# Head 1's keys and queries by seven products, the replaced block of x made in the gate stage, and weight sums in halves

## The chip, the cores and the metric

One NeuronCore of one Trainium2 chip runs the whole kernel. The metric is the device time of one launch in microseconds; a kernel's figure is the median of several executions. The engines are called PE (TensorE, matrix products), DVE (VectorE), ACT (ScalarE), POOL (GpSimd) and SP (SyncE). SP, ACT and POOL also issue transfers (DMAs); a queue's instructions run in order.

## What is computed

One layer of a hybrid decoder trunk on 512 tokens with 16 learned meta tokens ahead of them, all in float32, D = 2048:

```python
h = rms_norm(x, norm_w)
proj = h @ w_in
(dq, dk, dv, dz, db, da, gq, gk, gv, gz, gl, fq, fk, fv, fz, ff) = split_cols(proj)
...
o_dn = gated_head_norm(o_dn, dz, dn_norm_w)        # gated DeltaNet, 6 heads x 128
...
o_gla = gated_head_norm(o_gla, gz, gla_norm_w)     # GLA, 5 heads, keys 64, values 128
...
o_fox = o_fox.reshape(fz.shape) * silu(fz)         # forgetting attention, 5 heads x 128
o = concatenate([o_dn, o_gla, o_fox])[:, PAD:]
return x + o @ w_out
```

A final RMS norm follows, without the meta tokens. For this case the columns of `w_in` that matter most are fk, fq, fv and fz (keys, queries, values and gate of each attention head, a block of 128 columns each) and gz (the gates of the five GLA heads).

## The kernel before

**Exact products from two halves.** Each float32 weight block of 2048 x 128 comes in two raw tiles of 128 x 1024 (`load_half`, L144). SP loads the tile (L147), ACT casts it to a shorter format, `whi` (L165), and DVE subtracts to get the rest, `wlo` (L166); x is held as `xh` and `xl` in the same way, 16 tiles of 128 x 528 tokens. A projection (`inproj`, L254, with matmuls at L240) adds three products: whi x xh, whi x xl, wlo x xh. A block is 48 matmuls of 512 tokens, or 96 of 264 where the meta tokens are needed. Raw, whi and wlo tiles have two buffers each, so a half's split can begin when the half before the last is through PE.

**Seven products for two blocks.** `inproj_pair` (L558) makes two blocks together with seven half-size products (L571), each 24 matmuls of 264 tokens and one weight tile, where a plain pair would need eight. Four of its weight tiles are sums of blocks (`ti`). They are made in DRAM by POOL's DMAs: copies (L492) and accumulating transfers (L490), listed by `in_jobs` and cut into steps by `steps_of` (L485). `load_half` hands them out as it goes: each load adds `rate` to a budget and each step costs 1 or 1.6. `AHEAD` (L1276) starts this after the first gates with a rate of 1.4. The sums for the output projection (`tw`) follow in the same list. Three token sums (t1, t2, t4) are made by `x_sums`. One product needs a "replaced" block: for the 264 upper tokens, x of channel tile k+8 less x of tile k, written over `xh` and `xl` of tile k (k < 8) by `x_last` (L542) once nothing else reads those columns. For each k it loads two blocks (POOL, L546), scales one (ACT, L548), combines (DVE, L549), casts (ACT, L553) and takes the rest (DVE, L554).

**The order of the work.** DeltaNet's two groups of heads come first, then the gz gates of GLA (five projections of 512 tokens, each followed by `gate_z`: evacuation on DVE, a clamp on POOL at L385, three steps on ACT, one product on DVE, all on tiles `zgz` and `stgz`). During these gates DVE runs the elimination of the second DeltaNet group, a string of small operations on the tile `ab` (L740, L742). Its result goes through DRAM: ACT issues `sc` (L744), then `iv` (L747) and `xm` (L749), which wait for `sc`. Then come the projections of GLA in three pairs of heads (`gla_pair`, L957), then head 0 of attention with plain projections, then head 1's keys and queries plain too (`fk`, `fq`, called at the end of head 0 in `fox_head`, L1150), then `x_last`, then seven pairs: head 1's values and gate, and two pairs for each of heads 2, 3 and 4. Then follows the output projection (`pa`, `pq`, `ps`, `pt`, `pr`).

**What sets the order.** A scheduler with a model of its own fixes each engine's order when the kernel is built. The table `PLACE` (L197) says behind which matmul of a projection the small score matmuls of GLA stand: `"pss23": (('fk', 1), 60)` puts those of pair 2, level 3, behind the 60th matmul of fk of head 1. `paced` (L172) fixes that a weight sum's DMA stands behind the current split on POOL's queue, without a wait on a semaphore.

Of the kernel before, what the change touches and what calls it, by code (L numbers as in the profile page):

```python
# [18 lines left out]
P = 128  # L19
# [17 lines left out]
SKIP = 1  # L37
# [45 lines left out]
def tile_hybrid_trunk(ctx, tc, xT, xtok, mtok, w_gate, w_in, w_out, w_dn, consts, lmask, fin_w, out, dbg=None):  # L83
# [13 lines left out]
    def row(name, dt=F32):  # L97
        return wk.tile([P, 3 + T], dt, tag="row", bufs=7, name=name)
# [94 lines left out]
    def part(name, n=512):  # L193
# [11 lines left out]
        "pg00": (('gk', 2), 60),  # L205
        "pss10": (('fk', 0), 84),
# [278 lines left out]
    def steps_of(jobs):  # L485

        nonlocal ready
        for kind, out_, in_ in jobs:
            if kind:
                paced(G.dma_start(out=out_, in_=in_, accum_op=ALU.add, max_dma_last_dim=2048))  # L490
            else:
                x = G.dma_start(out=out_, in_=in_)  # L492
                paced(x)
                if ready < 4:
                    ready += 1
                    tc.add_manual_dep(x.ins, maxes[0].name, mybir.DependencyInfo(
                        mybir.DependencyClass.NoSync, mybir.DependencyReason.DATA), reason="behind")
            yield 1.6 if kind else 1
# [42 lines left out]

    def x_last():  # L542

        for k in range(NK):
            r = row(f"xe{k}")[:, :T]
            nc.gpsimd.dma_start(out=r.rearrange("p (i t) -> p i t", i=2), in_=xT[:, k : k + 9 : 8, HT:])  # L546
            x12, x22 = r[:, :HT], r[:, HT:]
            A.activation(x12, x12, AF.Copy, scale=nwc[:, k : k + 1])  # L548
            x = V.scalar_tensor_tensor(out=x22, in0=x22, scalar=nwc[:, k + 8 : k + 9], in1=x12, op0=ALU.mult,  # L549
                                       op1=ALU.subtract)  # L550
            tc.add_manual_dep(x.ins, kqs[-1].name, mybir.DependencyInfo(
                mybir.DependencyClass.NoSync, mybir.DependencyReason.DATA), reason="behind")
            A.copy(xh[k][:, HT:], x22)  # L553
            V.tensor_tensor(out=xl[k][:, HT:], in0=x22, in1=xh[k][:, HT:].bitcast(F32), op=ALU.subtract)  # L554
# [3 lines left out]
    def inproj_pair(n, c1, c2, each=None):  # L558
# [6 lines left out]
        def product(p_, src, xx, first=False, cols=slice(0, HT)):  # L565

            third[0] += 1
            hi, lo = load_half(src, f"{b1}_{len(order)}", raws[0] if third[0] % 3 == 0 and 0 < n and h < FOX_HEADS - 1 else None)
# [7 lines left out]
            if each:  # L576
# [16 lines left out]
        product(a, ti[n, 2], xs_(up, hi_))  # L593
        A.copy(c2[:, hi_], a[:, :HT])
        V.scalar_tensor_tensor(out=c2[:, hi_], in0=d[:, :HT], scalar=-1.0, in1=c2[:, hi_], op0=ALU.mult,
                               op1=ALU.subtract)
# [3 lines left out]
        product(a, w_in[b2, 1], sums("t4"), cols=dead)  # L600
        A.activation(c2[:, dead], a[:, dead], AF.Copy, scale=-1.0)
# [355 lines left out]
    def gla_pair(p):  # L957
# [52 lines left out]
        def scores(s, li):  # L1010
# [8 lines left out]
            V.tensor_tensor(out=dv[:, :, 1, :], in0=gv[:, :, 1, :], in1=ref, op=ALU.subtract)  # L1019
# [7 lines left out]
            kqs.append(V.tensor_tensor(out=qxv[:, :, 1, :], in0=qv[:, :, 1, :], in1=dv[:, :, 1, :], op=ALU.mult).ins)  # L1027
# [122 lines left out]
    def fox_head(h):  # L1150
# [125 lines left out]
    AHEAD = {(0, -1): (1.4, (-1, -2, -3, -4, -5, -6, -7), (0, 1, 2, 3))}  # L1276
# [366 lines left out]
```

## Time and profile before

| | us |
|---|---|
| median of 3 runs (lowest, highest) | 1001.61 (999.29, 1006.35) |
| the profiled execution | 997.56 |
| its span, first to last instruction | 995.9 |
| granted TensorE clock in it | 0.997 |
| DVE, ACT, POOL busy | 666.8, 475.3, 249.0 |

The profiled execution is 4.05 us below the median, and 1.7 us of it lie outside its span. The page gives for each engine the busy time, its share of the span and the number of instructions; then groups of instructions by line of the program, tile and shape. In the waits, "A <- B: total, times, longest" says how long A's engine stood idle until B ended. In a timeline a row is start, duration, engine, line, operation, and in brackets the idle time ahead of it with what ended it. In the chain, a row is start, duration, and what ran; a DMA there lasts from its issue until its landing was seen.

### The profile page before, as it was taken

What the parts mean: (1) busy time and instruction counts of PE and PEld (TensorE: products, weight loads), DVE (VectorE), ACT (ScalarE), POOL (GpSimd) and SP (SyncE); (2) the same over time, 40 slices, a digit from 0 to 9 for tenths busy, and PEclk for the clock granted to TensorE, in tenths of its full rate; (3) what the DMA queues carried; (4) which work ended last, traced back from release to release, by engine and by line L of the source; (5) the groups of instructions that cost most, each with busy time, mean ns of one, the idle gap of its engine ahead of it and who ended that gap; (6) DMA issues with size and microseconds to landing.
All of it is one profiled execution on the core that took longest, in us unless ns stands there. A gap on an engine that the chain in (4) does not pass through costs nothing.

```text
span 995.9 us, 19769 instructions
## 1 busy us (share of the span) xinstructions
PE 980.4 (98%) x7774; PEld 896.6 (90%) x7774; DVE 666.8 (67%) x1443; ACT 475.3 (48%) x1043; POOL 249.0 (25%) x293
## 2 busy tenths in 40 slices
PE   9999999999999999999999999999999999999996
PEld 7899999899999888899999988799999998888885
DVE  6356786966567895434675847776766676877573
ACT  7653533334456234334546444555555554454353
POOL 0031423322233244301313223221221134000060
PEclk9999999999999999999999999999999999999998
DMA  9754666777547688844847866565454577355634
GB/s 346 263 193 168 210 216 238 172 181 173 116 113 169 140 215 198 298 130 144 209 143 190 186 178 178 176 200 161 168 172 135 182 267 273 106 190 199 202 106 169
DMA packets 67489, 186.05 MB, mean 187 GB/s; under 512 B 13725, under 2 KB 16973, under 8 KB 66692
## 3 DMA queue, kind: packets, MB, share of 16 engines
q1 hardware_dynamic: 41920, 121.86, 36.0%
q0 software_dynamic: 16576, 56.83, 23.9%
q10 hardware_dynamic: 8900, 6.10, 2.2%
q8 instruction: 61, 1.00, 0.4%
q14 instruction: 32, 0.26, 0.1%
HBM read 174.07 MB, written 56.69 MB: 232 GB/s over the span
## 4 chain that ended last, share of the span: by engine, by line
PE 70%; DVE 7%; DMA 5%; ACT 3%; issue 2%; POOL 1%; ACTq 0%; DVEq 0%; POOLq 0%
PE pp L240 28%; PE pp_a L571 8%; PE pa L1392 5%; PE pq L1392 4%; PE pt L1392 4%; PE ps L1392 2%; PE pp_b L571 2%; PE pp_d L571 2%; PE pp_c L571 2%; DVE wlo L166 2%; DMA sc<-ab 1%; DMA zd<-gqk 1%; PE pr L1392 1%; PE pss L1041 1%; ACT whi L165 1%
## 5 line engine op out<-in xcount | busy, mean ns | idle before, releaser
L240 PE MATMUL pp<-xh,wlo 128*128 128x264 f32 (+2 forms) x1120 | 272.9, 306 | 2.2 <-DVE wlo L166 2.2
L240 PE MATMUL pp<-xh,whi 128*128 128x264 f32 (+2 forms) x1120 | 273.9, 306 | 0.0
L240 PE MATMUL pp<-xl,whi 128*128 128x264 f32 (+2 forms) x1120 | 272.9, 306 | 0.0
L165 ACT CAST whi<-raw 128x1024 fp32r<-128x1024 f32 x131 | 137.1, 1047 | 157.0 <-PE pp L240 81.2
L166 DVE TENSOR_TENSOR wlo<-raw,whi 128x1024 fp32r<-128x1024 f32 x131 | 160.6, 1226 | 72.8 <-ACT whi L165 64.2
L240 PEld LDWEIGHTS pp<-xh,wlo 128*128 128x128 f32 x1120 | 182.6, 189 | 12.1 <-DVE wlo L166 3.6
L240 PEld LDWEIGHTS pp<-xh,whi 128*128 128x128 f32 x1120 | 182.6, 189 | 9.4 <-ACT whi L165 0.4
L240 PEld LDWEIGHTS pp<-xl,whi 128*128 128x128 f32 x1120 | 182.7, 189 | 8.9 <-issue 0.4
L385 POOL TENSOR_SCALAR stc<-cv 128x528 f32<-128x528 f32 (+1 forms) x18 | 28.9, 1607 | 144.9 <-DVE cv L613 124.4
L613 DVE SCALAR_TENSOR_TENSOR cv<-pb,cpk,cv 128x528 f32<-128x528 f32 (+1 forms) x54 | 41.1, 761 | 0.8
L1417 POOL TENSOR_TENSOR acc<-acc,fw 128x512 f32<-128x512 f32 x4 | 5.8, 1483 | 117.4 <-ACT sqf L1414 117.4
L571 PE MATMUL pp_a<-t,whi 128*128 128x264 f32 (+1 forms) x224 | 30.5, 284 | 0.0
L1392 PE MATMUL pa<-wloo,oh 128*128 128x512 f32 x72 | 28.7, 398 | 0.0
L571 PE MATMUL pp_a<-xh,whi 128*128 128x264 f32 x112 | 28.4, 288 | 0.0
L571 PEld LDWEIGHTS pp_a<-t,whi 128*128 128x128 f32 x224 | 27.9, 189 | 0.5
L1392 PE MATMUL pa<-whio,ol 128*128 128x512 f32 x72 | 28.4, 394 | 0.0
L571 PE MATMUL pp_a<-xl,whi 128*128 128x264 f32 x112 | 28.3, 287 | 0.0
L385 POOL TENSOR_SCALAR stdz<-zdz 128x512 f32<-128x512 f32 x6 | 11.3, 1885 | 62.1 <-DVE zdz L403 62.0
L165 ACT CAST whis<-raws 128x1024 fp32r<-128x1024 f32 x16 | 16.3, 1048 | 21.2 <-PE pq L1392 10.8
L166 DVE TENSOR_TENSOR wlos<-raws,whis 128x1024 fp32r<-128x1024 f32 x16 | 19.2, 1223 | 10.7 <-ACT whis L165 10.6
L1392 PE MATMUL pa<-whio,oh 128*128 128x512 f32 x72 | 26.0, 400 | 0.0
L740 DVE TENSOR_TENSOR ab<-ab 51x30 f32<-51x30 f32 (+14 forms) x60 | 21.2, 354 | 6.4 <-DMA ab<-scr 4.2
(509 smaller groups left out, 2138.6 us busy)
## 6 DMA issues: line engine op xcount, KB each, us to landing
raw<-in_w_in SPq DMA_DIRECT2D x103, 512.0 KB, 3.7
ti<-in_w_in POOLq DMA_DIRECT2D x42, 512.0 KB, 5.5
raw<-ti SPq DMA_DIRECT2D x28, 512.0 KB, 3.3
tw<-in_w_dn POOLq DMA_DIRECT2D x24, 512.0 KB, 5.9
ti<-ti POOLq DMA_DIRECT2D x14, 512.0 KB, 6.3
rawo<-in_w_out SPq DMA_DIRECT2D x13, 512.0 KB, 3.2
raws<-tw SPq DMA_DIRECT2D x12, 512.0 KB, 3.9
xt<-in_xtok SPq DMA_DIRECT2D x8, 512.0 KB, 8.9
```

What stands on the lines that cost most here:

```text
L165: pace[0] = A.copy(hi, raw).ins
L166: pace[1] = V.tensor_tensor(out=lo, in0=raw, in1=hi.bitcast(F32), op=ALU.subtract).ins
L240: mm = PE.matmul(p_[:, :nt], wt[:, j * m : (j + 1) * m], xx[k][:, t0 : t0 + nt], start=(k == 0 and wt is hi and xx is xh), stop=(k == KT - ...
L385: maxes.append(G.tensor_scalar_max(t, src, LOW).ins)
L571: m = PE.matmul(p_[:, cols], wt[:, j * P : (j + 1) * P], xx[j][part_][:, cols], start=first and i == 0, stop=i == len(todo) - 1, skip_grou ...
L613: V.scalar_tensor_tensor(out=c, in0=pb[:, t0 + w : w + T], scalar=cwc[:, blk, w : w + 1], in1=c, op0=ALU.mult, op1=ALU.add)
L740: V.tensor_tensor(out=t3, in0=a3[:, j + 1 :, j : j + 1].to_broadcast([NN * 4 + H, m, j]), in1=a3[:, j : j + 1, 0:j].to_broadcast([NN * 4 + ...
L1041: mm = PE.matmul(ps[o0 : o0 + n, b * n : b * n + n], kx[rr, k0 : k0 + n], qx[rr, q0 : q0 + n], start=True, stop=True)
L1392: mm = PE.matmul(p_, o_[:, s], w_, start=(first and n == 0), stop=(last and n == 2), skip_group_check=True)
L1417: G.tensor_tensor(out=acc[tb, cc], in0=acc[tb, cc], in1=fw[cc], op=ALU.mult)
```

## The change

- `SKIP` goes from 1 to 0: head 1's keys and queries are made by seven products too, as pair 0 of now eight. In that pair the replaced product comes last, the product of the dead columns has a bank of its own, and the third raw buffer serves from pair 2 on.
- The replaced blocks are made in `x_early`, two, two, two, one and one after the five gz gates, and stored by POOL to a DRAM tile `x3`. `x_last` is now 16 loads from `x3`, called behind the matmuls of fz of head 0.
- Each DMA of a weight sum becomes two of 64 rows each, and each half waits on a semaphore for the DVE half of the split beside it (`pace[1]`). The rate becomes 1.65, steps cost 0.5 and 0.8, and an eighth pair is in the list.
- `PLACE` moves the scores of GLA's third pair of heads into attention's pair 1.

```diff
-SKIP = 1
+SKIP = 0
...
+        "pss21": (('pair', 1), 22),
...
+        "pss26": (('pair', 1), 102),
+        "pg02": (('pair', 1), 118),
...
-        "pss23": (('fk', 1), 60),
-        "pss24": (('fk', 1), 80),
-        "pss25": (('fk', 1), 90),
-        "pgo2": (('pair', 0), 8),
...
-            if kind:
-                paced(G.dma_start(out=out_, in_=in_, accum_op=ALU.add, max_dma_last_dim=2048))
-            else:
-                x = G.dma_start(out=out_, in_=in_)
-                paced(x)
...
-            yield 1.6 if kind else 1
+            for s in (slice(0, 64), slice(64, P)):
+                if kind:
+                    x = G.dma_start(out=out_[s], in_=in_[s], accum_op=ALU.add, max_dma_last_dim=2048)
+                else:
+                    x = G.dma_start(out=out_[s], in_=in_[s])
...
+                tc.add_manual_dep(x.ins, pace[1].name, mybir.DependencyInfo(
+                    mybir.DependencyClass.Sync, mybir.DependencyReason.DATA), reason="paced")
+                yield 0.8 if kind else 0.5
...
+    x3 = drp.tile([NK, P, T], F32, name="x3")
+
+    def x_early(k):
+
+        r, c = row(f"xe{k}")[:, :T], row(f"xc{k}", F32R)[:, :T]
+        nc.gpsimd.dma_start(out=r.rearrange("p (i t) -> p i t", i=2), in_=xT[:, k : k + 9 : 8, HT:])
+        x12, x22 = r[:, :HT], r[:, HT:]
+        A.activation(x12, x12, AF.Copy, scale=nwc[:, k : k + 1])
+        V.scalar_tensor_tensor(out=x22, in0=x22, scalar=nwc[:, k + 8 : k + 9], in1=x12, op0=ALU.mult,
+                               op1=ALU.subtract)
+        A.copy(c[:, :HT], x22)
+        V.tensor_tensor(out=c[:, HT:], in0=x22, in1=c[:, :HT].bitcast(F32), op=ALU.subtract)
+        nc.gpsimd.dma_start(out=x3[k], in_=c.bitcast(F32))
+
     def x_last():
 
         for k in range(NK):
-            r = row(f"xe{k}")[:, :T]
...
-            A.copy(xh[k][:, HT:], x22)
-            V.tensor_tensor(out=xl[k][:, HT:], in0=x22, in1=xh[k][:, HT:].bitcast(F32), op=ALU.subtract)
+            for x, o in ((xh, 0), (xl, HT)):
+                nc.gpsimd.dma_start(out=x[k][:, HT:].bitcast(F32), in_=x3[k][:, o : o + HT])
...
-            hi, lo = load_half(src, f"{b1}_{len(order)}", raws[0] if third[0] % 3 == 0 and 0 < n and h < FOX_HEADS - 1 else None)
+            hi, lo = load_half(src, f"{b1}_{len(order)}", raws[0] if third[0] % 3 == 0 and 1 < n and h < FOX_HEADS - 1 else None)
...
+        if n > 0:
+            product(a, w_in[b2, 1], sums("t4"), cols=dead)
+            A.activation(c2[:, dead], a[:, dead], AF.Copy, scale=-1.0)
+        else:
+            e = bank("e")
+            product(e, w_in[b2, 1], sums("t4"), True, cols=dead)
+            A.copy(c2[:, dead], e[:, dead])
+            replaced()
+            V.scalar_tensor_tensor(out=c2[:, dead], in0=a[:, dead], scalar=-1.0, in1=c2[:, dead],
+                                   op0=ALU.mult, op1=ALU.subtract)
...
         if h < H1:
...
+            done["fz", h] = inproj(("fz", h), meta=False)
+            x_last()
             gate_z("fz", h)
-            evac(inproj(("fk", H1)), ahead_[H1][:, 0])
-            evac(inproj(("fq", H1), meta=False), ahead_[H1][:, 2], scale=float(P) ** -0.5)
-            x_last()
             claim(h + 1)
...
-    AHEAD = {(0, -1): (1.4, (-1, -2, -3, -4, -5, -6, -7), (0, 1, 2, 3))}
+    AHEAD = {(0, -1): (1.65, (-1, -2, -3, -4, -5, -6, -7, -8), (0, 1, 2, 3))}
...
         gate_z("gz", h)
+        for i in ((0, 1), (2, 3), (4, 5), (6,), (7,))[h]:
+            x_early(i)
```

By the two orders, PE has 48 matmuls fewer of 512 columns, 48 more of 264 and 24 more of 248. There are three raw loads and splits more. Weight sums take 192 DMAs of half the size where there were 88.

The two orders differ most in the stage of the gz gates. First ACT's queue there, before: `whi` is the cast of a weight tile, `stgz` a gate's three steps, `sc`, `iv` and `xm` the way of the elimination through memory.

```order
L165 CAST whi_0_4873<-raw_0_4871 128x1024
L165 CAST whi_1_4904<-raw_1_4902 128x1024
L386 ACTIVATE stgz_4863<-stgz_4863 128x512
L744 DMA sc_4143<-ab_4071 51x1024
L387 ACTIVATE stgz_4863<-stgz_4863 128x512
L388 ACTIVATE stgz_4863<-stgz_4863 128x512
L165 CAST whi_0_4951<-raw_0_4949 128x1024
L747 DMA iv_4145<-sc_4143 128x12x32
L749 DMA xm_4147<-sc_4143 32x3x32
L165 CAST whi_1_5006<-raw_1_5004 128x1024
```

The same place after the change:

```order
L165 CAST whi_1_4950<-raw_1_4948 128x1024
L554 ACTIVATE xe_4817<-xe_4817,cpk 128x264
L557 CAST xc_4818<-xe_4817 128x264
L165 CAST whi_0_5000<-raw_0_4998 128x1024
L389 ACTIVATE stgz_4892<-stgz_4892 128x512
L390 ACTIVATE stgz_4892<-stgz_4892 128x512
L391 ACTIVATE stgz_4892<-stgz_4892 128x512
L165 CAST whi_1_5033<-raw_1_5031 128x1024
L554 ACTIVATE xe_4899<-xe_4899,cpk 128x264
L557 CAST xc_4900<-xe_4899 128x264
L767 DMA sc_4205<-ab_4133 51x1024
L165 CAST whi_0_5089<-raw_0_5087 128x1024
```

Ahead of nearly every `whi` of these gates now stands a block's scale (`xe`) and cast (`xc`), whose inputs come by a DMA and through DVE. The two issues behind `sc` are followed by a block too:

```order
L770 DMA iv_4207<-sc_4205 128x12x32
L772 DMA xm_4209<-sc_4205 32x3x32
L554 ACTIVATE xe_4907<-xe_4907,cpk 128x264
L557 CAST xc_4908<-xe_4907 128x264
L165 CAST whi_1_5145<-raw_1_5143 128x1024
```

POOL's queue in the same stage, before, with the clamps (`stgz`) and the accumulating transfers (`ti`):

```order
L385 TENSOR_SCALAR stc_4065<-cv_4060 128x512
L385 TENSOR_SCALAR stgz_4648<-zgz_4646 128x512
L490 DMA ti<-ti 256x512 x2
L385 TENSOR_SCALAR stgz_4719<-zgz_4717 128x512
L490 DMA ti<-ti 256x512 x2
L385 TENSOR_SCALAR stgz_4791<-zgz_4789 128x512
L490 DMA ti<-ti 256x512 x2
L385 TENSOR_SCALAR stgz_4863<-zgz_4861 128x512
```

And after:

```order
L559 DMA x_683<-xc_4720 128x528
L494 DMA ti<-ti 128x512 x2
L388 TENSOR_SCALAR stgz_4802<-zgz_4800 128x512
L552 DMA xe_4809<-in_xT 128x2x264
L559 DMA x_683<-xc_4728 128x528
L494 DMA ti<-ti 128x512 x2
L552 DMA xe_4817<-in_xT 128x2x264
L559 DMA x_683<-xc_4810 128x528
L494 DMA ti<-ti 128x512 x2
L388 TENSOR_SCALAR stgz_4892<-zgz_4890 128x512
L552 DMA xe_4899<-in_xT 128x2x264
L559 DMA x_683<-xc_4818 128x528
```

The loads of blocks (`xe`) and the stores (`x_683`, which is the tile `x3`, each behind DVE's last operation on its block) stand between the clamps, with two halves of a sum beside each.

DVE's queue at the end of the elimination, after the change, where L763 and L765 are the elimination's two operations:

```order
L763 TENSOR_TENSOR ab_4133<-ab_4133 51x58
L765 TENSOR_TENSOR ab_4133<-ab_4133 51x2x29
L558 TENSOR_TENSOR xc_4900<-xe_4899,xc_4900 128x264
L763 TENSOR_TENSOR ab_4133<-ab_4133 51x30
L765 TENSOR_TENSOR ab_4133<-ab_4133 51x30
L166 TENSOR_TENSOR wlo_0_5090<-raw_0_5087,whi_0_5089 128x1024
L555 SCALAR_TENSOR_TENSOR xe_4907<-xe_4907,cpk 128x264
L406 TENSOR_TENSOR zgz_4980<-pp_0_4915,rstd 128x512
L558 TENSOR_TENSOR xc_4908<-xe_4907,xc_4908 128x264
L166 TENSOR_TENSOR wlo_1_5146<-raw_1_5143,whi_1_5145 128x1024
```

The operations on `xe` and `xc` of the blocks 0 to 4 (ten of them) stand ahead of its last step, and the evacuation `zgz_4980` has moved behind it.

More of the change, by code (lines that the diff above doesn't have):

```diff
@@ L592, in inproj_pair, with replaced @@
         V.tensor_tensor(out=c1[:, hi_], in0=d[:, :HT], in1=c1[:, hi_], op=ALU.add)
[L593 to L596, printed above, removed]
+        def replaced():
+            product(a, ti[n, 2], xs_(up, hi_))
+            A.copy(c2[:, hi_], a[:, :HT])
+            V.scalar_tensor_tensor(out=c2[:, hi_], in0=d[:, :HT], scalar=-1.0, in1=c2[:, hi_], op0=ALU.mult,
+                                   op1=ALU.subtract)
+        if n > 0:
+            replaced()
         c = bank("c")
@@ L599, in inproj_pair @@
         V.tensor_tensor(out=c1[:, hi_], in0=c[:, :HT], in1=c1[:, hi_], op=ALU.add)
-        product(a, w_in[b2, 1], sums("t4"), cols=dead)
-        A.activation(c2[:, dead], a[:, dead], AF.Copy, scale=-1.0)
+        if n > 0:
+            product(a, w_in[b2, 1], sums("t4"), cols=dead)
[4 more added lines that the diff above has]
+            A.copy(c2[:, dead], e[:, dead])
+            replaced()
+            V.scalar_tensor_tensor(out=c2[:, dead], in0=a[:, dead], scalar=-1.0, in1=c2[:, dead],
+                                   op0=ALU.mult, op1=ALU.subtract)
     def conv_silu(key, blk, dst, meta=True):
@@ L1018, in scores @@
             ref = gv[:, :, 0, s - 1 : s].to_broadcast([R, npair, s])
-            V.tensor_tensor(out=dv[:, :, 1, :], in0=gv[:, :, 1, :], in1=ref, op=ALU.subtract)
+            x = V.tensor_tensor(out=dv[:, :, 1, :], in0=gv[:, :, 1, :], in1=ref, op=ALU.subtract)
+            if p == 2 and li == 0:
+                kqs.append(x.ins)
             if s > 1:
```

21 lines of the change are left out of this document (9 added, 12 removed).

## Prediction

> **What bounds the kernel now.** I read the page's busy times first, then TensorE's waits, and then the two stretches that the change touches. The page's first row:
>
> ```profile
> PE 980.4 (98%) x7774; PEld 896.6 (90%) x7774; DVE 666.8 (67%) x1443; ACT 475.3 (48%) x1043; POOL 249.0 (25%) x293
> ```
>
> TensorE is busy for 980.4 of 995.9 us. The list of what it waited for, whole:
>
> ```profile
> PE pp L240 <- DVE wlo L166: 2.2, 4, 0.7
> PE pss L1041 <- DVE kq L1027: 1.3, 3, 0.9
> PE pss L1041 <- issue: 1.3, 2, 0.7
> PE warm L304 <- POOL ones L114: 1.2, 1, 1.2
> PE pk L673 <- DVE kT L389: 1.0, 2, 0.8
> PE pp L309 <- ACT xh L297: 0.3, 1, 0.3
> ```
>
> That is 7.3 us, all that better timing alone could win: 0.7%. A gain of over 1% (10 us, about what a measurement of this kernel can tell from no change) would need matmul work to go as well, and little of it goes. But TensorE's work is a queue fed by splits (a cast on ScalarE, a subtraction on VectorE), so anything that makes a split late is paid in full. The question is therefore what the new work does to the splits.
>
> **The columns.** Matmuls stand in the chain with their pace, 512 columns first, then 264:
>
> ```profile
> 904.16 11.11 PE ps L1392 x48
> ```
> ```profile
> 720.00 2.94 PE pp_b L571 x24
> ```
>
> So 0.2315 us for 512 columns and 0.1225 for 264. By the two orders the change removes 48 matmuls of 512 columns (fq of head 1, 48 x 0.2315 = 11.1 us) and has 48 more of 264 and 24 more of 248 (seven products of 24 where fk had 96). I price the 248 like 264, a bound from above: 72 x 0.1225 = 8.8. Term: **-2.3 us**, on the path, since TensorE is never idle there.
>
> **The old place of the replaced block, 616 to 655.** Before, eight blocks of x were made there. The chain at that place, then TensorE:
>
> ```profile
> 623.62 5.71 DMA xe<-in_xT
> ...
> 630.45 0.95 ACT whi L165
> ```
> ```profile
> 631.79 0.39 PE L240 MATMUL pp<-xl,whi 128*128 128x512 f32 x1
> 632.71 0.50 PE L240 MATMUL pp<-xh,wlo 128*128 128x512 f32 x1 [0.53 <-DVE wlo L166]
> 633.04 0.40 PE L240 MATMUL pp<-xh,whi 128*128 128x512 f32 x1
> 633.66 0.46 PE L1041 MATMUL pss<-kq 64*32 64x32 f32 x32 [0.22 <-DVE kq L1027]
> 634.33 0.46 PE L1041 MATMUL pss<-kq,kq 64*32 64x32 f32 x32 [0.22 <-DVE kq L1027]
> ```
>
> ScalarE, in order, waited for a block to land and cast the weights after it. TensorE's starts are 0.92 and 0.62 us apart where 0.23 was due, then 0.67 against 0.39 (634.33 to the next start at 634.72): about 0.7 + 0.4 + 0.3. All three go, with what caused them. Term: **-1.4 us**.
>
> In its stead stand 16 loads of 128x264 from memory on POOL's queue, behind the matmuls of fz0 whose operand they overwrite. Their product is the seventh of pair 0, 6 x 2.94 = 17.6 us later. The nearest row is the issue of a block (below, 0.72 us) and its landing, 5.1: 16 x 0.72 + 5.1 = 16.6, and the last block is used 14 matmuls (1.7 us) into the product. Hidden, with 2.7 us to spare. Cost 0; with the longest landing, 6.8, still 0. POOL's clamp of fz0's gate waits behind these issues, some 12 us, but its gate is needed only at the end of head 0's attention.
>
> **The seven products of head 1's keys and queries** come with two raw buffers (the third serves from pair 2 on). Rows of a split:
>
> ```profile
> L165 ACT CAST whi<-raw x131: 1031/1049/1079, 44.0 to 808.5; 128x1024 fp32r<-128x1024 f32 x131
> L166 DVE TENSOR_TENSOR wlo<-raw,whi x131: 1189/1221/1648, 45.1 to 809.5; 128x1024 fp32r<-128x1024 f32 x131
> ...
> DMA to landing us min/median/max: 3.1/3.6/8.6
> ```
>
> A buffer's round is 3.6 + 1.05 + 1.22 and some 0.3 of handing over, 6.2 us, and serves every second product, 5.9. Seven products lose 3.5 x 0.3 = 1.0 us of lead. A product's wlo is first used 16 matmuls in, 2.0 us of slack, and pair 1, which now carries the scores of GLA's third pair of heads, gives time back. Cost 0, at most 1. The extra evacuations (one on VectorE, three on ScalarE) lie beside matmuls there: the page has VectorE at 67%.
>
> **The stretch of the GLA gates, 345 to 400,** where the blocks are made now. VectorE there, in two windows (busy time of PE, PEld, DVE, ACT, POOL, then clock, DMA share and GB/s):
>
> ```profile
> 348.00:384.00 36.00, 36.00 (x158) 29.30 (x157) 33.16 (x74) 13.57 (x18) 16.56 (x11) 1.00 0.92 218
> 384.00:400.00 16.00, 15.49 (x103) 14.16 (x102) 6.51 (x14) 8.09 (x13) 8.49 (x9) 1.00 0.73 190
> ```
>
> VectorE is busy for 33.2 of 36 us: it runs the elimination of `ab`, a string of small operations that each wait for the last, with splits between (the page's group of one of its two operations):
>
> ```profile
> L740 DVE TENSOR_TENSOR ab<-ab 51x30 f32<-51x30 f32 (+14 forms) x60 | 21.2, 354 | 6.4 <-DMA ab<-scr 4.2
> ```
>
> The elimination's end is followed by a trip through memory, first in ScalarE's timeline, then in the chain (this group of heads, then the first group), then in TensorE's timeline:
>
> ```profile
> 393.45 0.39 ACTq L747 DMA_DIRECT2D iv<-sc  x1
> 393.87 0.68 ACTq L749 DMA_DIRECT2D xm<-sc  x1
> 394.65 1.05 ACT L165 CAST whi<-raw 128x1024 fp32r<-128x1024 f32 x1 [7.13 <-issue]
> ```
> ```profile
> 384.63 8.81 DMA sc<-ab
> ```
> ```profile
> 209.14 5.70 DMA sc<-ab
> ```
> ```profile
> 397.01 0.52 PE L240 MATMUL pp<-xh,wlo 128*128 128x264 f32 x2 [0.51 <-DVE wlo L166]
> ```
>
> The reader is to see that a weight cast stands on ScalarE behind two issues that wait for `sc`, and that TensorE already stalls 0.51 us for it: the cover is used up. Whatever ends `ab` later is paid.
>
> Now the price of a block, by the same instructions at their old place (tile `xe`; the last line is its landing), and of what POOL's queue holds beside it:
>
> ```profile
> L546 POOL DMA_DIRECT2D xe<-in_xT x8: 722/723/825, 616.7 to 642.6; - x8
> L548 ACT ACTIVATE xe<-xe,cpk x8: 501/515/517, 621.8 to 651.4; 128x264 f32<-128x264 f32 x8
> L549 DVE SCALAR_TENSOR_TENSOR xe<-xe,cpk x8: 479/484/1048, 637.9 to 652.7; 128x264 f32<-128x264 f32 x8
> L553 ACT CAST xh<-xe x8: 395/412/414, 638.4 to 653.2; 128x264 fp32r<-128x264 f32 x8
> L554 DVE TENSOR_TENSOR xl<-xe,xh x8: 419/424/434, 639.7 to 653.7; 128x264 fp32r<-128x264 f32 x8
> ...
> DMA to landing us min/median/max: 3.2/5.1/6.8
> ```
> ```profile
> L490 POOL DMA_DIRECT2D ti<-ti x14: 882/946/1272, 295.1 to 384.5; - x14
> ```
> ```profile
> ti<-ti POOLq DMA_DIRECT2D x8, 512.0 KB, 7.5
> ```
> ```profile
> L385 POOL TENSOR_SCALAR stgz<-zgz x5: 1487/2477/2700, 350.2 to 391.1; 128x512 f32<-128x512 f32 x5
> ```
>
> First effect: splits behind landings. In the changed order each block's scale and cast (ScalarE) stand ahead of a half's weight cast, in nearly every half of gates 1 to 4. A half is 24 x 0.2315 = 5.56 us; its split may start at the boundary before and needs 1.05 + 1.22 + 0.1, and wlo is first used 0.46 into it: slack 5.56 + 0.46 - 2.4 = 3.6 us. POOL's order ties block k+2 to block k: store of k (issue 0.72, as a load), two halves of a sum (0.95 each, the price of a whole, a bound from above), one clamp in every other half, load of k+2 (0.72 + 5.1), then 0.52 + 0.48 + 0.41. That is 12.3 us with the clamp, against a gate's 11.1: 1.2 us of lead lost in each of four gates, 4.8 in all, of which 3.6 are slack. Stall 1.2; VectorE, already full, adds waiting at each handover (two per block, up to one 0.35 us step of `ab` each), and I take **2.0**. Bounds: with the shortest landing, 3.2, the round is 10.4 and nothing is lost; with the longest, 6.8, 2.9 x 4 - 3.6 = 8.0.
>
> Second effect: `ab` ends later. Ten operations on five blocks stand ahead of its last step, 5 x (0.48 + 0.42) = 4.5 us, and one evacuation of 0.67 has moved behind it: 3.9 us of work in a stretch with 2.8 idle, most of it early. So `sc` is issued at about 388 instead of 384.6; lands after 5.7 to 8.8; two issues 1.1; a block's handover 1.4 to 1.5 (new, ahead of the cast); split 2.4. wlo stands at 398.7 to 401.8. It was needed at 396.5, at 398.5 with the 2.0 above. Stall 0.2 to 3.3, of which I take the middle, 1.7, in place of 0.5 now. Both effects: 2.0 + 1.7 - 0.5 = **+3.2 us**, between -0.5 and 8.0 + 3.3 - 0.5 = 10.8.
>
> **The sums in halves.** 88 transfers become 176, 16 more come with the eighth pair, and each waits for the subtraction of the split beside it in the code. What is queued behind a half on POOL is the clamp of a gate (needed by ScalarE, which sits ahead of a weight cast) and the next block; both are worked in above. Total issue by the rows' prices stays under a third of POOL's time, and the sums are done far ahead of their use in both orders. Cost on the path 0; a gain comes only by a block landing sooner behind a half than behind a whole. Here the Trainium skill, page "DMA: Bandwidth & Descriptors", section "Rules for kernel authors", speaks against the change: of two transfers to disjoint partition halves it says "Don't bother — they serialize". By it a block that stands behind two halves waits as behind one whole, and what that would make of the time is the second rival; the trace has no halves, and so can't say yet.
>
> **Sum.** -2.3 - 1.4 + 3.2 = -0.5 against the profiled execution: 997.56 to about 997.1. That execution lies 4.05 below the median of the runs shown (1001.61), so the median comes to about **1001 us**. The GLA scores that move into pair 1 and the attention heads that end half a pair later change places among matmuls without new ones, and are costed at nothing: the output projection's first 50 us take them in.
>
> **The rivals.**
> - The blocks are hidden. Landings near 3.2, `sc` in 5.7. For it: ScalarE is busy for only 13.6 of 36 us there. Against it: the DMA share of 0.92 and 8.81 for the last `sc`. Time: 997.56 - 3.7 = 993.9, as a median 998.
> - Landings become the bound (the other side). A block lands as a whole sum does there, in 7.5: the round is 14.7, 3.6 lost per gate, 3.6 x 4 - 3.6 = 10.8, and 3.3 behind `sc`: +13.6 after the 0.5, so 997.56 - 3.7 + 13.6 = 1007.5, median 1011.5. It decides from about 6.5, where gates lose over 2.6 each. For it: DMA share 0.92. Against it: the sums are spread thinner here.
> - The change doesn't do what it says: the replaced block comes late after all, because POOL reaches its 16 loads behind paced sums or a landing takes over 8 us. Then pair 0 stalls 3 to 5 us: median about 1005.
>
> **How the numbers follow.** Likeliest, as summed: 0.47, own range 998 to 1005. Hidden: 0.28 (996 to 999). Landings the bound: 0.18. Late block: 0.07. The range of 995 to 1011 leaves out half of the third case and little else, so 0.12 or so; the runs' own spread (999.29 to 1006.35) is inside it. Faster by over 1% (below 991.6) needs more than the columns and all stalls of the two places: 0.03. Slower by over 1% (above 1011.6): the upper half of the landing case and a part of the unknown, 0.13. Within 1%: 0.84.
>
> **What would show it.** Columns: TensorE's busy time falls by 2 to 3 us. Old place: no idle of TensorE behind fz0, no `xe` in ScalarE's waits near 630. Gates: TensorE waits for `wlo` between 360 and 405 by some 3.7 us in all, ScalarE waits for `xe` before weight casts, and `sc` is issued near 388. Pairs 0 and 1: no wait of a matmul for `wlo` over 0.3. I am wrong if TensorE stalls nowhere in the gates (first rival), if those stalls pass 8 us (second), or if a wait stands in the seventh product of pair 0 (third).

## The result, and the profile after

The changed kernel took 1045.98 us (median of six, 1038.55 to 1050.69) against 1000.25 before. The ratio is 1.0447 with a 95% interval of 1.04 to 1.0494. It is some 46 us slower, far outside the predicted range of 995 to 1011. The profiled execution, 1050.69, is the slowest of the six; its span is 53 us longer than that of before.

The page's busy times after:

```profile
PE 999.6 (95%) x7798; PEld 914.5 (87%) x7798; DVE 665.5 (63%) x1449; ACT 480.8 (46%) x1050; POOL 329.0 (31%) x422
```

Of a span of 1048.9, TensorE is idle for 49.3 us where it was 15.5: 33.8 more. But its busy time has grown too, by 19.2 us, although by the prices of the prediction its matmuls are 2.3 us less. So 33.8 + 19.2 = 53.0 is the whole difference, and some 21.5 us of it (19.2 + 2.3) is the same work done more slowly. The granted clock accounts for it: the busy time times what the clock lacks of 1.00, summed over windows of 1 us, is 20.5 us in the changed kernel and 0.0 in the kernel before. TensorE's waits, the longest of 18 rows:

```profile
PE pp L243 <- DVE wlo L166: 9.7, 5, 5.3
PE pp L243 <- ACT whi L165: 5.7, 3, 2.8
PE pm L782 <- DVE iv L776: 3.6, 1, 3.6
PE psd L1029 <- ACT gvt L973: 3.2, 1, 3.2
PE pp_a L582 <- ACT fqk L596: 3.0, 1, 3.0
PE pa L1418 <- DVE acc L1433: 2.8, 1, 2.8
```

Before there were six rows and none over 2.2. By stage, these waits come to 5.3 us near 92, 3.6 near 228, 9.6 in the gate stage (350 to 450), 10.5 in the GLA stage (450 to 600), 4.2 from there to 700, 3.0 near 717 and 3.4 after 800. The gate stage, the only place where I forecast new stalls, has a fourth of them.

Where the slower work comes from is seen behind one stall. Windows of the changed kernel around the one near 92 (busy time of PE, PEld, DVE, ACT, POOL; then the granted clock, the DMA share and GB/s):

```profile
80.00:90.00 10.00, 10.00 (x84) 9.82 (x83) 3.59 (x7) 2.96 (x6) 3.79 (x5) 1.00 0.73 255
90.00:96.00 6.00, 0.98 (x9) 0.72 (x7) 3.69 (x15) 1.81 (x4) 0.00 (x0) 0.94 0.03 13
96.00:102.00 6.00, 5.71 (x26) 5.71 (x27) 4.39 (x8) 1.46 (x2) 3.13 (x7) 0.50 0.67 232
102.00:108.00 6.00, 6.00 (x50) 6.00 (x50) 3.26 (x6) 2.88 (x4) 2.89 (x6) 0.99 0.80 263
```

TensorE waits 5.3 us, and in the next 6 us it runs 26 matmuls at a clock of 0.50 where 50 follow in the 6 us after that. A stall of this length is paid twice.

Four links of the chain that ended last in the gate stage show the mechanism that I had forecast, larger:

```profile
370.84 7.93 DMA xe<-in_xT
...
385.60 10.18 DMA xe<-in_xT
...
406.57 11.17 DMA sc<-ab
417.77 0.39 ACTq L770
```

These two blocks land in 8 and 10 us (the median of all eight is 6.4, where I had 5.1); `sc` lands in 11.2, not 8.8. POOL's own waits in the changed kernel, the costliest for each kind of sum, and the clamp's; then the clamp's before:

```profile
POOL ti L496 <- DVE wlo L166: 56.6, 17, 11.3
...
POOL ti L494 <- DVE wlo L166: 44.4, 13, 12.0
POOL tw L494 <- DVE wlo L166: 40.5, 10, 10.8
...
POOL stc L388 <- DVE cv L636: 14.5, 10, 2.5
```
```profile
POOL stc L385 <- DVE cv L613: 124.4, 14, 15.4
```

POOL stands for over 140 us in front of sums that wait for a split. Before, no sum waited for one, and POOL stood idle for 124 us in all for the clamp `stc`; now for 14.5, since POOL arrives late. What queues behind is shown by the chain in the GLA stage, where x's loads for the token sums stand on POOL:

```profile
522.24 0.44 POOL tw L494
...
523.56 6.51 DMA xa<-in_xT
530.09 0.51 ACT xa L539
530.61 0.48 ACT gvt L973
...
531.13 0.28 PE pwg L975
```

A sum was held for a split, the load of `xa` went out behind it, ScalarE waited for the load, and behind ScalarE's scaling of it waited a copy that TensorE needed.

### The profile page after: what moved, and what is told of

It reads as the page before. It is cut to its first block, busy times and chain, and to the rows that moved or that the text cites. A ratio compares the mean times of both kernels' runs of the same rounds, so it can differ in the third digit from the quotient of the medians.

```text
span 1048.9 us, 20079 instructions
## 1 busy us (share of the span) xinstructions
PE 999.6 (95%) x7798; PEld 914.5 (87%) x7798; DVE 665.5 (63%) x1449; ACT 480.8 (46%) x1050; POOL 329.0 (31%) x422
## 4 chain that ended last, share of the span: by engine, by line
PE 69%; DMA 15%; DVE 7%; ACT 4%; issue 3%; POOL 2%; ACTq 0%; SPq 0%; DVEq 0%; POOLq 0%
PE pp L243 27%; PE pp_a L582 7%; PE pp L312 4%; PE pq L1418 4%; PE pt L1418 4%; PE pa L1418 3%; DVE wlo L166 2%; DMA eg<-gd 2%; PE ps L1418 2%; PE pp_c L582 2%; DMA xe<-in_xT 2%; PE pp_b L582 2%; PE pp_d L582 2%; DMA sc<-ab 2%; DMA xb<-in_xT 2%
## 5 line engine op out<-in xcount | busy, mean ns | idle before, releaser
L243 PE MATMUL pp<-xh,wlo 128*128 128x264 f32 (+2 forms) x1072 | 266.6, 312 | 10.4 <-DVE wlo L166 9.7
L243 PE MATMUL pp<-xh,whi 128*128 128x264 f32 (+2 forms) x1072 | 265.7, 311 | 5.8 <-ACT whi L165 5.7
L243 PE MATMUL pp<-xl,whi 128*128 128x264 f32 (+2 forms) x1072 | 267.6, 312 | 0.0
L165 ACT CAST whi<-raw 128x1024 fp32r<-128x1024 f32 x134 | 140.4, 1048 | 165.0 <-PE pp L243 86.2
L166 DVE TENSOR_TENSOR wlo<-raw,whi 128x1024 fp32r<-128x1024 f32 x134 | 164.4, 1227 | 68.9 <-ACT whi L165 60.3
L496 POOL DMA_DIRECT2D ti<-in_w_in x64 | 31.8, 502 | 56.9 <-DVE wlo L166 56.6
L494 POOL DMA_DIRECT2D ti<-in_w_in x32 | 29.4, 1097 | 50.7 <-DVE wlo L166 34.0
L494 POOL DMA_DIRECT2D ti<-ti x32 | 28.5, 1078 | 25.6 <-DVE wlo L166 10.4
L388 POOL TENSOR_SCALAR stc<-cv 128x528 f32<-128x528 f32 (+1 forms) x18 | 29.7, 1651 | 19.8 <-DVE cv L636 14.5
L582 PEld LDWEIGHTS pp_a<-t,whi 128*128 128x128 f32 x240 | 31.1, 196 | 3.5 <-ACT fqk L596 3.2
L582 PE MATMUL pp_a<-xh,whi 128*128 128x264 f32 x128 | 32.1, 285 | 0.6 <-ACT vf L600 0.6
L582 PE MATMUL pp_a<-xl,whi 128*128 128x264 f32 x128 | 32.5, 288 | 0.0
```

The source lines that it names most:

```text
L165: pace[0] = A.copy(hi, raw).ins
L166: pace[1] = V.tensor_tensor(out=lo, in0=raw, in1=hi.bitcast(F32), op=ALU.subtract).ins
L243: mm = PE.matmul(p_[:, :nt], wt[:, j * m : (j + 1) * m], xx[k][:, t0 : t0 + nt], start=(k == 0 and wt is hi and xx is xh), stop=(k == KT - ...
L388: maxes.append(G.tensor_scalar_max(t, src, LOW).ins)
L494: x = G.dma_start(out=out_[s], in_=in_[s], accum_op=ALU.add, max_dma_last_dim=2048)
L496: x = G.dma_start(out=out_[s], in_=in_[s])
```

## The experiments

After the result I had three theories. W: the waits hold POOL's queue, and x's loads behind them are late. X: the blocks made in the gates cost it, as in my rivals. T: the denser traffic of sums slows other transfers. Two came later, P and S: the seven products of head 1 cost by the places of the GLA scores, or by the rate at which they want weights. The ratios are to runs of the kernel before in the same session (medians 998.0 to 1000.3); where I compare runs of two sessions, I take what each lies above its own kernel before:

| run | what differs | us | ratio, 95% interval |
|---|---|---|---|
| changed kernel | | 1045.98 | 1.0447 (1.040 to 1.0494) |
| e18_whole_wait | changed, whole sums that wait | 1047.08 | 1.0478 (1.0443 to 1.0513) |
| e1_halves_free | changed, halves without waits | 1026.4 | 1.0277 (1.0238 to 1.0316) |
| e2_whole_sums | changed, whole, no waits | 1017.47 | 1.0197 (1.0146 to 1.0248) |
| e5_after_block_late | changed, blocks made late | 1035.56 | 1.0372 (1.0329 to 1.0415) |
| e6_rate14 | changed, rate 1.4 | 1033.13 | 1.0338 (1.031 to 1.0367) |
| e7_pair_only | seven products, table, rate 1.65 | 1019.4 | 1.0208 (1.0155 to 1.0261) |
| e9_pair_only_rate14 | e7 at rate 1.4 | 1016.15 | 1.0175 (1.0138 to 1.0213) |
| e12_pair_place | e9 with the old places | 1011.1 | 1.013 (1.0086 to 1.0175) |
| e14_early_whole_place | e12 with early blocks | 1011.55 | 1.0121 (1.0079 to 1.0162) |
| e16_pair_sums_done | e12, sums done sooner | 1017.51 | 1.0148 (1.0104 to 1.0192) |
| e8_before_blocks_early | before, early blocks | 1001.62 | 1.0032 (1.0016 to 1.0048) |
| e4_before_halves_free | before, halves | 1009.37 | 1.0111 (1.0067 to 1.0154) |
| e3_before_halves_wait | before, halves that wait | 1009.67 | 1.0107 (1.0064 to 1.015) |
| e15_before_rate165 | before, rate 1.65 | 1004.02 | 1.004 (1.0013 to 1.0067) |
| e19_before_rate165_wait | e15, whole sums that wait | 1017.12 | 1.0166 (1.0121 to 1.0211) |
| e17_before_rate12 | before, rate 1.2 | 1000.8 | 1.0016 (0.9998 to 1.0034) |
| e10_three_stalls | before, three stalls put in | 1023.87 | 1.026 (1.0236 to 1.0284) |

**The wait and the size of a sum.** Two edits of the changed kernel and their opposite make a square. The first removes the wait. What is left is an order alone, as for whole sums before: a half stands on POOL's queue behind the cast of its split.

```diff
-                tc.add_manual_dep(x.ins, pace[1].name, mybir.DependencyInfo(
-                    mybir.DependencyClass.Sync, mybir.DependencyReason.DATA), reason="paced")
+                paced(x)
```

> The changed kernel with its sums still in halves, but each half only placed behind its split on POOL's queue, as whole sums were before, with no semaphore wait. Theory W (the waits hold POOL's queue, so that the loads of x behind them are issued late and ScalarE, in order, holds the weight casts): most of the loss goes, about 1005 to 1020 us. Theory X (the blocks made in the gate stage cost it): 1035 to 1045, as the waits aren't what matters. Theory T (denser traffic of the sums): 1035 to 1045.

The second puts back the loop of before, whole and without waits; the third is that with the wait added to each whole transfer.

```diff
-            for s in (slice(0, 64), slice(64, P)):
...
+            if kind:
+                paced(G.dma_start(out=out_, in_=in_, accum_op=ALU.add, max_dma_last_dim=2048))
+            else:
+                x = G.dma_start(out=out_, in_=in_)
+                paced(x)
...
+            yield 1.6 if kind else 1
```

> The changed kernel with whole sums again, placed as before and without waits (steps cost 1 and 1.6, rate still 1.65). Theory W: as with free halves, 1005 to 1020; if halving by itself costs something, below that run. Theory X: 1035 to 1045. Theory T: 1035 to 1045 or more.

> The changed kernel with whole sums that keep the semaphore wait. With the three others (halves and waits 1046, halves free 1026, whole free 1017) it completes a square. If the wait costs 20 whatever the size of a transfer: 1035 to 1040. If it costs for each transfer that waits: 1025 to 1030. If only halves with waits hold POOL's queue: 1015 to 1020.

Without waits the changed kernel lies 19 us (whole) and 28 (halves) above the kernel before, with them 48 and 46. The wait costs 18 (halves) and 29 (whole); halving costs 9 where nothing waits, and nothing more where everything waits. The runs with free halves and with whole sums that wait came out above all that I expected of them. Theory W stands as the largest single part, and it was no matter of halves. Waits and halves together are 27 of 46 us; the rest remains without them.

Where the wait costs is seen by setting the profiled changed kernel beside e1, whose span is 25.1 us shorter: 11.8 us of that is idle time and 13.3 is TensorE's busy time. In the GLA stage TensorE's waits are nearly the same, 10.0 us in e1 and 10.5 in the changed kernel. But e1's longest there is 1.5 us, and its clock stays at 1.00; in the changed kernel the longest is 3.2 us, and the clock falls to 0.50 twice in that stage.

**The same on the kernel before.**

> The kernel before with nothing changed but the sums: in halves, each with the semaphore wait (rate 1.4, steps 0.5 and 0.8). Theory W: 1020 to 1035, with POOL idle behind its sums' DMAs for over 100 us and TensorE waiting behind late loads of x. Theory X and theory T: 998 to 1005.

> The kernel before with its sums in halves, placed behind their splits but without the semaphore wait (the run with the wait took 1009.7 against 998.4). If the wait is what costs there: 997 to 1002. If the halving by itself costs (twice as many issues on POOL, each ahead of a load of x): 1005 to 1010.

Both missed what theory W said: 1009.7 with the wait, 1009.4 without. At the rate of before the wait costs nothing on halves, although POOL stands for 193 us in front of them in e3, more than in the changed kernel; the halving alone costs 11 us. Almost all of that lies at two spots. TensorE's waits of e4:

```profile
PE pp L240 <- DVE wlo L166: 6.0, 2, 5.6
PE pm L760 <- DVE iv L754: 3.0, 1, 3.0
```

The chain of e4 around the two, in two answers:

```profile
85.19 9.09 DMA gb<-gd
```
```profile
218.11 5.50 DMA sc<-ab
223.63 7.62 DMA iv<-sc
```

A split stood behind the landing of `gb` on VectorE, and the first group's elimination handed over 9 us later than before (`sc` at 218.1, where it was 209.1), of which the stall at the first spot is 5.6 and the slower clock behind it (0.50 from 96 to 102) some 3. That the halves made both late through POOL's 88 further issues is argued, not shown by a run of its own.

So why does the wait cost 18 and more in the changed kernel? Three runs look at the rate:

```diff
-    AHEAD = {(0, -1): (1.65, (-1, -2, -3, -4, -5, -6, -7, -8), (0, 1, 2, 3))}
+    AHEAD = {(0, -1): (1.4, (-1, -2, -3, -4, -5, -6, -7, -8), (0, 1, 2, 3))}
```

> The changed kernel, whole as it is (halves, waits, early blocks, eight pairs), with the rate of the sums at 1.4 in place of 1.65. If the waits cost because more transfers than loads stand between two splits (rate): 1020 to 1030. If they cost because the early blocks and x's loads queue behind them whatever the rate: 1038 to 1048.

> The kernel before with whole sums at the rate 1.65 (1004 without waits) that wait on their splits. If the wait costs through the rate: 1015 to 1025. If it costs only with the changed kernel's early blocks and eighth pair: 1002 to 1008.

> The kernel before with the rate of the sums at 1.65 and nothing else. If denser sums delay the transfers of the first stages: 1001 to 1005, with TensorE idle for some 3 us more between 85 and 105. If the rate costs only where other things are late already: 997 to 1000.

At 1.65 the wait alone takes the kernel before from 6 us above its unchanged runs to 17, where at 1.4 the wait on halves cost nothing; and the changed kernel loses 12 us less at 1.4, though not as much as I expected. So the wait costs through the rate in part: more sums stand between two splits, and what lies behind them leaves later. ScalarE's wait for x's loads shows it, in the kernel before at 1.65 without the wait, then with it; then in the changed kernel at 1.65 and at 1.4:

```profile
ACT xa L534 <- DMA xa<-in_xT: 5.9, 2, 5.0
```
```profile
ACT xa L535 <- DMA xa<-in_xT: 31.2, 5, 8.7
```
```profile
ACT xa L539 <- DMA xa<-in_xT: 28.8, 5, 9.3
```
```profile
ACT xa L539 <- DMA xa<-in_xT: 12.8, 5, 6.6
```

At 1.65 the same wait costs whole sums 12 us in the kernel before and 29 in the changed kernel. What the early blocks and the eighth pair add to it, no run separates, and whole sums that wait at 1.4 were not tried.

The rate alone cost 4 us by the ratio (1.3 to 6.7), 5.7 by the medians, theory T's size. Thinner sums were tried against the suspicion that any order but the tuned one is worse:

> The kernel before with the rate of the sums at 1.2 in place of 1.4. Theory T (denser sums delay the transfers on which DeltaNet's first group waits): thinner sums are no slower there, TensorE idle between 85 and 105 and near 225 at most as before; what then remains of the sums in the first pairs can cost up to 3: 997 to 1002. Theory F (the order at 1.4 was chosen with the chip and every other order is worse, denser or thinner): 1003 to 1008, with the same stalls as at 1.65.

1000.8 against 999.3, no difference that can be measured. Not every other order is worse: the one thinner rate isn't, the denser ones are.

**The blocks.** In the first of these runs the blocks are made late, as before, in the changed kernel; in the second they are made early in the kernel before.

```diff
-        for i in ((0, 1), (2, 3), (4, 5), (6,), (7,))[h]:
-            x_early(i)
...
     def x_last():
 
         for k in range(NK):
-            for x, o in ((xh, 0), (xl, HT)):
-                nc.gpsimd.dma_start(out=x[k][:, HT:].bitcast(F32), in_=x3[k][:, o : o + HT])
+            r = row(f"xe{k}")[:, :T]
...
```

> The changed kernel without the early blocks: the replaced block is made as before, from x, behind the projection of fz of head 0 (seven products for head 1's keys and queries, halves and waits stay). Theory X: 1005 to 1020. Theory W: 1030 to 1045, since only the stalls of the gate stage go, some 11 us with what the clock takes. Theory T: 1035 to 1045.

> The kernel before with only the early blocks: made after the gz gates, stored to memory, loaded by 16 transfers where they were made before; sums whole and without waits. The prediction's term for the gate stage, with what the clock takes after a stall: TensorE idle there by 3 to 7 us, in all 1002 to 1010. Rival (landings are short when no halves hold POOL's queue, so blocks are hidden): 996 to 1000.

Late blocks save 8 to 10 us in the changed kernel. Alone, early blocks cost 3.6 us (1.6 to 4.8 by the interval). In e8 the blocks also leave their old place, so by my sum that figure stands against 3.2 - 1.4 = 1.8. TensorE's waits in e8:

```profile
PE pp L240 <- DVE wlo L166: 4.3, 6, 1.6
PE pp L240 <- ACT whi L165: 2.4, 3, 1.3
...
PE pn L799 <- DVE uf L788: 1.5, 1, 1.5
```

From 340 to 410 the first two come to 4.8 us, where 0.5 stood before: 4.3 for my term of 3.2. So the blocks aren't hidden, as the first rival had it. None of e8's waits is longer than 1.6 us, the clock stays at 1.00 up to its last microseconds, and its busy time, 980.3, is that of before.

**Seven products alone.** What remains when sums, waits and blocks are as before (the first of the two runs still has the rate of 1.65):

> Head 1's keys and queries by seven products and nothing else of the change but its table and its rate: whole sums placed as before, no waits on them, the replaced block made late from x. If the costs found so far simply add (waits and halves 28, blocks 10), about 1007 us, with what is left due to the seven products' own stage, the moved GLA scores and the rate. If the parts overlap, so that one late queue hides another, 1010 to 1017. If the seven products cost nothing by themselves, as the prediction had it, 996 to 999.

> The run with seven products alone, with the rate of the sums at 1.4 again in place of 1.65. If the denser traffic of sums delays other transfers in the first stages (the run with whole sums idled 2 to 3 us more between 90 and 105 and as much near 228 than the kernel before): 3 to 6 us below that run. If the rate is idle: the same within 2.

1019 and 1016, 21 and 18 us above the kernel before: this part, which I had at nothing to 1 us, costs some 18 by itself. (The profiled executions of these two were their fastest, 1010.73 and 1009.34, so a part of it is in no trace.) Two things are seen in e9. In the first pairs the chain runs through four weight loads, of which these are the first and the last:

```profile
616.17 7.27 DMA raw<-ti
...
647.67 6.19 DMA raw<-ti
```

That belongs to the rate of 1.4, at which the longer list of sums runs into these pairs. In the changed kernel, at 1.65, the sums are done by then, and the same loads land in 3.4 us (median, 650 to 700):

```profile
raw<-ti SPq DMA_DIRECT2D x8, 512.0 KB, 3.4
```

TensorE's waits in its first pairs come to 2.2 us, where e9 has 6.4.

And in e9 TensorE has two waits at places where the changed kernel waits too, in the third pair and at the output projection's start:

```profile
PE pp_a L588 <- ACT fqk L602: 2.6, 1, 2.6
PE pa L1422 <- ACT whio L165: 2.3, 1, 2.3
```

The next run puts the GLA scores back to their old distance from head 0's last projection; the one after adds the early blocks.

```diff
-        "pss21": (('pair', 1), 22),
...
-        "pg02": (('pair', 1), 118),
+        "pss23": (('pair', 0), 60),
+        "pss24": (('pair', 0), 80),
+        "pss25": (('pair', 0), 90),
+        "pgo2": (('pair', 1), 26),
```

> The run of seven products alone at rate 1.4 (1016.2), with the scores of GLA's third pair of heads put back to where they stood against the end of head 0's last projection: levels 3, 4 and 5 behind 60, 80 and 90 matmuls of pair 0 and the output behind 26 of pair 1. Theory P (the table's places cost: pair 0 has no other TensorE work to give two raw buffers time, and attention ends later, into the output projection): 1003 to 1009, with the idle of pairs 0 and 1 and the 2.5 us stall at the output projection's start gone. Theory S (the seven products' own stage is slow: raw loads land in 6 to 7 us beside the blocks' loads, whatever stands between): 1013 to 1018.

> The changed kernel with whole sums without waits, rate 1.4, and the places of the run before: the blocks are made early, so no loads of x lie beside pair 0. Theory P and theory S together: raw loads in pair 0 land in 3.5 to 5 us, the gate stage stalls by 3 to 5, 1001 to 1006. Theory P alone: 1005 to 1010.

1011.1, between the two ranges: by the medians the places were 5 us, and both waits are gone. But the intervals of e9 and e12 overlap, and their profiled executions took 1009.3 and 1009.7, so what the places cost is likely and not shown. Early blocks change nothing there (1011.6, more than I expected). What is left in e12's profile is in pair 0: some 7 us of waits, and behind the longest, 3.5 us, a mean clock of 0.66 from 640 to 655. The DMAs from 610 to 660 in e12, then the weights in the kernel before from 630 to 665:

```profile
tw<-tw POOLq DMA_DIRECT2D x8, 512.0 KB, 8.5
raw<-ti SPq DMA_DIRECT2D x7, 512.0 KB, 7.1
```
```profile
raw<-ti SPq DMA_DIRECT2D x5, 512.0 KB, 3.7
```

The sums of the output projection run into the pair, and its weights land in 7.1 us, not 3.7. A run with sums that are done by then:

```diff
-    AHEAD = {(0, -1): (1.4, (-1, -2, -3, -4, -5, -6, -7, -8), (0, 1, 2, 3))}
+    AHEAD = {(0, -1): (1.4, (-1, -2, -3, -4, -5, -6, -7, -8), (0, 1, 2, 3)), ("g", 0): (2.2,)}
```

> The run of seven products alone with the old places (1011.1), with the rate of the sums raised from 1.4 to 2.2 from the first GLA pair on, so that the last sum of the output projection's weights is issued before head 1's first pair, not during it. Theory S, made narrower (in the first pair each product wants a new weight tile every 2.9 us, and the raw loads land in 6 to 8 us because accumulating sums share the DMA engines): raw loads land in 4 to 5 there, the idle of that pair falls from about 8 to under 3 us, 1002 to 1006. If the blocks' own loads are what slows them: 1009 to 1013.

The weights then land in 3.9:

```profile
raw<-ti SPq DMA_DIRECT2D x6, 512.0 KB, 3.9
```

But the time is 1017.5 (1007.0 to 1019.3), not 1002 to 1006: the pair still idles (1.7 and 1.4 us at two products), and stalls of 4.7 us at 405 and 2.5 at 588 are new; that the denser sums cause them is argued. In e7 the weights land in 3.4 too, and it takes 1019. So the loads are slow where the sums run beside them, but quick loads alone don't bring the time back. Whether the third raw buffer would have served pair 0 wasn't tried.

**The clock.** Three weight loads of the kernel before were made to wait until TensorE had finished the half before.

```diff
+        if name in [f"{BLOCK_OF[b]}_1" for b in (("dv", 4), ("gv", 1), ("fv", 0))]:
+            tc.add_manual_dep(ld, order[-1].name, mybir.DependencyInfo(
+                mybir.DependencyClass.Sync, mybir.DependencyReason.DATA), reason="stall")
```

> The kernel before with three stalls put in: the second weight load of three projections (values of DeltaNet head 4, of GLA head 1, of attention head 0) waits until TensorE has finished the first half. By rows of the split each leaves TensorE idle for about 3.6 + 1.05 + 1.22 = 5.9 us, less what the third buffer or order hides. If idle time costs itself alone: three times 5.9, 1016 us, and TensorE's busy time as before, 980. If the clock drops after an idle of this length, as 0.53 to 0.68 in the windows behind the stalls of the changed kernel: busy time 6 to 13 us higher, 1022 to 1029 in all.

TensorE's busy time in it, for the same matmuls as before, then the windows around the third stall:

```profile
PE 988.8 (97%) x7774; PEld 904.2 (89%) x7774; DVE 662.4 (65%) x1443; ACT 477.3 (47%) x1043; POOL 256.5 (25%) x293
```
```profile
583.00:589.00 6.00, 0.74 (x5) 0.53 (x5) 0.80 (x4) 1.04 (x1) 0.00 (x0) 0.95 0.50 175
589.00:595.00 6.00, 5.97 (x113) 5.13 (x115) 2.95 (x4) 1.05 (x1) 0.00 (x0) 0.50 0.54 172
595.00:601.00 6.00, 6.00 (x114) 5.45 (x99) 0.92 (x4) 3.13 (x8) 2.95 (x4) 0.98 0.36 107
```

Busy time 8.4 us higher and 1023.9 in all: idle time doesn't cost itself alone. The other 17.2 of the span's 25.6 us are idle time. After 5.3 us without matmuls the clock stands at 0.50 for about 6 us. TensorE's waits at the three places came to 3.7 (in three parts), 2.6 (in two) and 5.3 us, less than worked out, and the order has moved elsewhere too (4.9 us of idle at the output projection that I had not put in), so the 8.4 are for four stalls, not three. The Trainium skill, page "TensorE: Matmul & The Clock Gate", section "Part 1: The HAM clock gate (the "warmup" mystery)", says that the clock is at half after about 3.4 us of idle; the 0.50 agrees. The length doesn't quite: over the traces of all runs, the clock fell to 0.50 behind each of the 25 waits of TensorE of 3.0 us or longer, but also behind 34 of the 53 between 1.5 and 3.0 us. In e9 a wait of 2.3 us at the output projection's start is followed by 3.4 us at 0.50.

## Why the prediction was wrong, point by point

- **What bounds the kernel.** That a late split is paid in full was right. It is paid in more than full: I priced stalls at their own length, and the clock added some 21.5 of 53 us in the profiled execution. No step of the sum had a term for it.
- **"The sums in halves. ... Cost on the path 0."** This step failed most. I counted that POOL has time to spare, and that a wait behind a split is over soon. The runs show some 27 us: the wait makes POOL late, not busy, and x's loads and the clamps stand behind it in order. I asked what is queued behind a half, named the clamp and the next block, and left out the loads of `xa` and `xb` in the GLA stage, where a fourth of TensorE's waits and two of the drops of the clock lie in the changed kernel. How the 27 us divide among the stages is not shown. The Trainium skill, page "DMA: Bandwidth & Descriptors", section "Rules for kernel authors", says of two transfers to disjoint partition halves not to bother; the halves here are rows of tiles in memory, and they did worse than gain nothing: halving alone cost 9 and 11 us.
- **"The seven products ... Cost 0, at most 1."** It cost some 18 us in the runs with this part alone. The term of a raw buffer's round, 3.6 + 1.05 + 1.22, had the median landing of all 131 loads. At the rate of 1.65 that was right (3.4 in the changed kernel, whose first pairs wait 2.2 us, not at most 1); at 1.4 the landing there is 6 to 7, since the stage's own traffic decides it. The larger waits lie where I looked for none: 3.0 us in the third pair and 2.8 at the output projection's start. What makes up the rest of the 18 is open.
- **"costed at nothing: the output projection's first 50 us take them in."** The moved scores and the later attention brought two stalls of 2.3 and 2.6 us (e9), which are gone with the old places (e12). By the medians that is 5 us, within what the two runs' intervals leave open.
- **The rate.** The sum had no term for 1.65 against 1.4. It cost 4 to 6 us alone, and the changed kernel is 12 us faster at 1.4 (e6). But 1.65 also keeps the sums out of the first pairs, so neither rate is free.
- **The gates, +3.2.** Near enough alone: 4.3 by the waits in e8. In the changed kernel TensorE waits 9.6 us in the stage, 5.1 in e1 without POOL's waits: sums that wait stand ahead of the blocks' loads, and the blocks land in 6.4 (median). That comes close to my second rival (a landing of 6.5, stalls over 8 us), and is a fourth of TensorE's waits.
- **The columns, -2.3, and the old place, -1.4.** The matmul counts are as worked out; no run shows the gain by itself, since clock and stalls cover it. At the old place TensorE waits 0.5 us in e8, where it was 0.9.
- **The third rival**, a late block, isn't seen: no wait of TensorE in the changed kernel is for the block's loads.

What stays open: what the seven products cost beyond their waits in the trace, what the blocks and the eighth pair add to the cost of the wait, and why the halves delay the first group on the kernel before. No version tried beats the kernel before.

## What to carry to other kernels

When one engine is busy 98% of the time, price each stall twice: by its length, and by the slower clock after it if it is long (here behind every wait of 3.0 us or longer, and two in three of those from 1.5 to 3.0). A semaphore wait on a queue that also issues loads costs what stands behind it, so list every instruction behind it to the next stage, not only those in the stage that you look at. Take a transfer's duration from the stage where it will run, with the traffic that will be there.

## What the runs showed of the hardware

- After 5.3 us of idle TensorE ran at 0.50 for about 6 us, in a stall put in by hand as in one that came by itself; after a single wait of 2.3 us (e9) it ran at 0.50 for 3.4 us. The clock fell so behind all 25 waits of 3.0 us or longer in the traces, and behind 34 of 53 from 1.5 to 3.0.
- A weight tile of 512 KB landed in 3.7 us (median, kernel before) and 3.4 (changed kernel) with no accumulating sums beside it, and in 7.1 (e12) with them, in the same stage.
- One program's executions can spread by 1.5%: the kernel before at rate 1.65 took 997 to 1012 us over ten runs.
